# Softmax dealt out in three stages, heads four steps apart, rotary in two steps, retention's first half behind attention

## Chip, cores and metric

One core of a Trainium2 chip runs the whole program. The metric is the device time of one execution in microseconds (us).

## What is computed

One block of a streaming encoder on 256 frames of width 2048: a half-step SwiGLU feed-forward, two token mixers side by side (chunked band attention, retention), gates that merge them, a second feed-forward, a last norm. What the change touches is in the mixers:

```python
h = rmsnorm(x, norm_mix_g)
q_a, k_a, v_a, q_r, k_r, v_r, g_r, gate_a, gate_r = split(h @ w_in)
# attention, 8 heads of 128, per head
p = softmax(where(valid, q_a @ k_a.T * 128**-0.5 + bias[rel_idx], -1e30))
att = p @ v_a
# retention, 8 heads of 128, per head and chunk
q_r, k_r = rotary(q_r), rotary(k_r)
s = (q_r @ k_r.T) * decay
ret = s @ v_r + (state part)          # then divided by its root mean square
ret = silu(g_r) * ret
merged = sigmoid(gate_a) * (att @ w_out_att) + sigmoid(gate_r) * (ret @ w_out_ret)
x = x + merged @ w_out
```

## The kernel before

All large products run in fp32 by three passes: weights and inputs are split into a high and a low half, and TensorE forms hi x hi, hi x lo and lo x hi. The work is a list of **steps**, each a 256-row chunk of a 512-column weight block (two pieces of 128 rows by two tiles of frames by three passes: 12 matmuls). SyncE's queue loads a chunk; `split` (L117 to L124) makes its halves: a cast on ScalarE (L121, `hi`) and a subtraction on VectorE (L122, `lo`). `run` (L220) goes through the steps in order. At step c it first issues the split of step c + 3 (four buffers for each half, `SPLIT_BUFS`), then the side work that is due at c, then the products of c. `later(n, fn)` (L104) puts a piece of side work n steps ahead; `at(step, fn)` puts it at a step. On TensorE a step thus reads [side work][12 products]; on ScalarE and VectorE [split of c + 3][side work]. Nothing reorders this afterwards: what the list says is each engine's order.

PSUM has six banks for the products (tags `acc` and `z`) and a ring of two for side work (`side_tile`, L90), so a third side tile waits until the first has been copied out.

The stretch that the change touches starts with step `mixed` (the second half of retention's value projection), eight steps; then come qr0, kr0, qr1, kr1, eight steps each, then the output projections. Its side work is:

- the relative bias: `set_bias` loads it transposed and, four steps on, turns it with sixteen transposes through four side tiles (`psb`, L325) which ScalarE copies out (L330). It starts at step `mixed`.
- attention, head by head: `scores` (two products `as`, L848, L849; then all of the softmax: scale and bias on VectorE L856, maxima L862, sign L863, the powers on ScalarE L865, reciprocal L868, multiplication L870), two steps later `transposes` (`apt`, L877, with a copy on ScalarE L879), two steps later `values` (`av`, L885, L886, with a split whose low half, `attl`, is on VectorE, L343). Heads are three steps apart; the first has its scores at `mixed` + 10.
- a finished q or k projection of retention: `ret_qk_done` has ScalarE move two tiles out of PSUM (L806), rotates both on VectorE at once (L815 to L818, six operations for each tile), and has them transposed three or four steps later (`qr0p` and the like, L348, copied out by ScalarE L783 and VectorE L785).
- retention, once per half (four heads): `scores` (`rs`, L908, L909; decay on VectorE L911, L912), two steps later `values` (`ro`, L921 to L923), heads two steps apart; one step behind the last `values` stands `finish`, the closing: square on ScalarE (L931), sum on VectorE (L933), reciprocal root with a power on GpSimd (L338, L339), gate on VectorE (L939).
- GpSimd's queue loads the gain of the second norm, gates and decay; the gain is turned by one narrow transpose (L263).

Of the kernel before, what the change touches and what calls it, by code (L numbers as in the profile page):

```python
# [10 lines left out]
AF = mybir.ActivationFunctionType  # L11
# [6 lines left out]
NT = SEQ // P  # L18
# [19 lines left out]
HALF_K = D // P // 2  # L38
LEAD = 12
MIX_LEAD = 8  # L40
HELD = 6

SHARE = (0.85,) * 4 + (1.0,) * 4 + (0.8,) + (0.4,) * 3 + (0.15,) * 4
# [27 lines left out]
def block_kernel(ctx: ExitStack, tc: tile.TileContext, x, g1, w1g, w1u, w1d, gm, w_in, rel, woa, wor, wo,  # L71
                 g2, w2g, w2u, w2d, gf, cos, sin, decay, ident, out):
    nc = tc.nc
# [19 lines left out]
    def tmp_tile(name, tag="t", bufs=None):  # L93
        return tmp.tile([P, NB], F32, tag=tag, name=name, bufs=bufs)
# [9 lines left out]
    def later(n, fn):  # L104
        due.setdefault(state["step"] + n, []).append(fn)
# [649 lines left out]
    nm = Norm("nm", gains[:, 1, :], True)  # L755
# [12 lines left out]
    scale = HD ** -0.5  # L768
# [31 lines left out]
    def ret_qk_done(key, b, after=None):  # L800
        def done(acc):
            srcs = []
            half = HD // 2
            for t in range(NT):
                s = tmp_tile(f"{key}{b}{t}", "gate", 2)
                nc.scalar.activation(s, acc[t], AF.Copy, scale=nm.scale(t))  # L806
                r = tmp_tile(f"{key}{b}{t}r", "qk", 4)
                u = tmp_tile(f"{key}{b}{t}u", "scaled", 1)
                s4 = s.rearrange("p (h j d) -> p h j d", h=4, j=2)
                r4 = r.rearrange("p (h j d) -> p h j d", h=4, j=2)  # L810
                u4 = u.rearrange("p (h j d) -> p h j d", h=4, j=2)
                c = cos_sb[:, t, :].unsqueeze(1).to_broadcast([P, 4, half])
                n = sin_sb[:, t, :].unsqueeze(1).to_broadcast([P, 4, half])
                for j in range(2):
                    nc.vector.tensor_mul(r4[:, :, j, :], s4[:, :, j, :], c)  # L815
                    nc.vector.tensor_mul(u4[:, :, j, :], s4[:, :, 1 - j, :], n)
                nc.vector.tensor_sub(r4[:, :, 0, :], r4[:, :, 0, :], u4[:, :, 0, :])
                nc.vector.tensor_add(r4[:, :, 1, :], r4[:, :, 1, :], u4[:, :, 1, :])  # L818
                srcs.append(r)
            to_transposed(key, b, srcs, 4 if after is None else 3)  # L820
            if after is not None:
                after()

        return done
# [15 lines left out]
    def attention(h):  # L840
        b, i = h // 4, h % 4
        hs = slice(i * HD, (i + 1) * HD)
        sm = {}

        def scores():
            q, k = tposed["qa", b], tposed["ka", b]
            ps = side_tile(f"as{h}")
            nc.tensor.matmul(ps[:, 0:SEQ], q[:, i, P:SEQ], k[:, i, :], start=True, stop=True)  # L848
            nc.tensor.matmul(ps[:, SEQ : SEQ + P], q[:, i, 0:P], k[:, i, 0:P], start=True, stop=True)  # L849
            room = act_tile(F32, f"p{h}").rearrange("p a q -> p (a q)")  # L850
            s = room[:, : 3 * P].rearrange("p (j k) -> p j k", j=3)
            sm["room"] = room
            p3 = ps[:, : 3 * P].rearrange("p (j k) -> p j k", j=3)

            for j, bj in ((0, 1), (1, 0), (2, 0)):
                nc.vector.scalar_tensor_tensor(  # L856
                    s[:, j, :], p3[:, j, :], scale, table["bias", b][:, i, bj * P : (bj + 1) * P], op0=ALU.mult, op1=ALU.add
                )
            m = small.tile([P, NT], F32, tag="m", name="m")
            tot = small.tile([P, NT], F32, tag="l", name="l")  # L860
            for t, js in ((1, slice(0, 2)), (0, slice(2, 3))):
                nc.vector.reduce_max(m[:, t : t + 1], s[:, js, :], axis=AX.XY)  # L862
            nc.vector.tensor_scalar_mul(m, m, -1.0)  # L863
            for t, js in ((1, slice(0, 2)), (0, slice(2, 3))):
                nc.scalar.activation(  # L865
                    s[:, js, :], s[:, js, :], AF.Exp, bias=m[:, t : t + 1], accum_out=tot[:, t : t + 1]
                )
            nc.vector.reciprocal(tot, tot)  # L868
            for t, js in ((1, slice(0, 2)), (0, slice(2, 3))):
                nc.vector.tensor_scalar_mul(s[:, js, :], s[:, js, :], tot[:, t : t + 1])  # L870
            sm["p"] = s

        def transposes():
            ps = side_tile(f"apt{h}")

            for j, c in ((2, 0), (0, 1), (1, 2)):
                nc.tensor.transpose(ps[:, c * P : (c + 1) * P], sm["p"][:, j, :], id_sb)  # L877
            pt = sm.pop("room")[:, 3 * P : 6 * P]
            nc.scalar.copy(pt, ps[:, : 3 * P])  # L879
            sm["pt"] = pt  # L880

        def values():
            v = nat["va", b]
            ps = side_tile(f"av{h}")
            nc.tensor.matmul(ps[:, :SEQ], v[:, 0, hs], sm["pt"][:, :SEQ], start=True, stop=False)  # L885
            nc.tensor.matmul(ps[:, P:SEQ], v[:, 1, hs], sm["pt"][:, SEQ:], start=False, stop=True)  # L886
            hi, lo = att.alloc(b)
            split_out(ps[:, :SEQ], hi[:, i, :], lo[:, i, :])

        return scores, transposes, values  # L890

    def all_attention():
        for h in range(HEADS):
            for s, stage in enumerate(attention(h)):
                later(2 + 3 * h + 2 * s, stage)

    def retention(b):
        outs = {}

        def head(i):  # L900
            h = 4 * b + i
            hs = slice(i * HD, (i + 1) * HD)
            sm = {}

            def scores():
                q, k = tposed["qr", b], tposed["kr", b]
                ps = side_tile(f"rs{h}")
                nc.tensor.matmul(ps[:, 0:SEQ], k[:, i, 0:P], q[:, i, :], start=True, stop=True)  # L908
                nc.tensor.matmul(ps[:, SEQ : SEQ + P], k[:, i, P:SEQ], q[:, i, P:SEQ], start=True, stop=True)  # L909
                s = act_tile(F32, f"rp{h}").rearrange("p a q -> p (a q)")[:, : 3 * P]  # L910
                nc.vector.tensor_mul(s[:, :SEQ], ps[:, :SEQ], table["decay", b][:, i, :])  # L911
                nc.vector.tensor_mul(s[:, SEQ:], ps[:, SEQ : SEQ + P], table["decay", b][:, i, 0:P])  # L912
                sm["s"] = s

            def values():
                if i == 0:
                    for t in range(NT):
                        outs[t] = acc_tile(f"ro{b}{t}", ("acc", "z")[t])
                v = nat["vr", b]
                s = sm["s"]  # L920
                nc.tensor.matmul(outs[0][:, hs], s[:, 0:P], v[:, 0, hs], start=True, stop=True)  # L921
                nc.tensor.matmul(outs[1][:, hs], s[:, P:SEQ], v[:, 0, hs], start=True, stop=False)
                nc.tensor.matmul(outs[1][:, hs], s[:, SEQ:], v[:, 1, hs], start=False, stop=True)  # L923

            return scores, values

        def finish():
            srcs = []
            for t in range(NT):
                sq = tmp_tile(f"rsq{b}{t}", "gate", 2)  # L930
                nc.scalar.activation(sq, outs[t], AF.Square)  # L931
                ms = small.tile([P, 4], F32, tag="ms", name="ms")
                nc.vector.reduce_sum(ms, sq.rearrange("p (h d) -> p h d", h=4), axis=AX.X)  # L933
                rs = small.tile([P, 4], F32, tag="rs", name="rs")
                rsqrt(rs, ms, HD, 4)
                o = tmp_tile(f"rg{b}{t}", "qk", 4)
                for i in range(4):
                    hs = slice(i * HD, (i + 1) * HD)
                    nc.vector.scalar_tensor_tensor(  # L939
                        o[:, hs], outs[t][:, hs], rs[:, i : i + 1], nat["gr", b][:, t, hs], op0=ALU.mult, op1=ALU.mult  # L940
                    )
                srcs.append(o)
            later(3, lambda: [ret.put(b, t, srcs[t]) for t in range(NT)])

        for i in range(4):
            for s, stage in enumerate(head(i)):
                later(5 + 2 * i + 2 * s, stage)
        later(5 + 2 * 4, finish)

    w_in0 = w_in[0]  # L950

# [35 lines left out]
    mixed = len(steps)  # L987
# [14 lines left out]
    merges, of_ret = [], []  # L1002
# [72 lines left out]
    def at(step, fn):  # L1075
        due.setdefault(step, []).append(fn)
# [3 lines left out]
    turn = load_gain(g1, 0, nc.scalar)  # L1080
# [45 lines left out]
    mix = next(c for c, s in enumerate(steps) if s.job.w is w_in0)  # L1126
    at(mix - 18, load_rel)
    at(mix - 14, lambda: later(4, load_gain(gm, 1)))
    at(mixed, set_bias)
    at(mixed + 8, all_attention)  # L1130
    at(mixed + 8, lambda: later(8, load_gain(g2, 2)))
    at(mixed + 16, load_ret_gates)
    at(mixed + 20, set_decay)
    for step, fn in merges:
# [65 lines left out]
```

## Time and profile before

| | |
|---|---|
| median of 3 runs | 2115.38 us (2114.66 to 2119.7) |
| profiled execution | 2116.28 us, span 2114.5 us |
| TensorE busy | 2070.1 us (98% of the span) |
| VectorE busy | 1761.4 us (83%) |
| ScalarE busy | 1407.0 us (67%) |
| GpSimd busy | 273.5 us (13%) |
| mean granted clock of TensorE | 0.996 |

The span runs from the first to the last instruction; the profiled execution's time lies 1.8 us above it. Busy times are over the whole program; the stretch of the change is 1060 to 1280 of the span. In a row of the timeline stand the start, the time of the group, engine, line and operation, output and inputs, their shapes, and in brackets how long the engine had been idle before it and what it waited for. A granted clock of 1.00 is 2.4 GHz, 0.5 is 1.2 GHz.

### The profile page before, as it was taken

Reading aid. Unit: us, or ns where it says so; the run is one execution under the profiler, and the core shown is the slowest. Engines: PE = TensorE matmul, PEld = TensorE weight load, DVE = VectorE, ACT = ScalarE, POOL = GpSimd, SP = SyncE. Lnnn points to the kernel's source line nnn. Section 1 sums busy time; section 2 is a strip of 40 time slices with the busy share of each in tenths; the row PEclk is TensorE's granted clock in tenths of the full one; section 3 lists DMA queues with packets and bytes.
Section 4 is the critical chain, followed back from the end, with each engine's and each line's share of the span. In section 5 each row is a group of like instructions: output and inputs, shape, how many; then the busy total and the mean of one; then the engine's idle time right before and its main releaser. Section 6 shows DMA issues by size and latency. Waiting matters only on the chain. (4 is left out here: it accounts for less than half of the span.)

```text
span 2114.5 us, 25819 instructions
## 1 busy us (share of the span) xinstructions
PE 2070.1 (98%) x9256; PEld 1691.4 (80%) x9256; DVE 1761.4 (83%) x1825; ACT 1407.0 (67%) x1734; POOL 273.5 (13%) x322
## 2 busy tenths in 40 slices
PE   9999999999999999999998999999999999999998
PEld 7788878878888888878787788887888878888886
DVE  6998899889997799888856567568889988898986
ACT  7677667767777766766664334556676677677785
POOL 1111211122111111112100000010121012110200
PEclk9999999999999999999999999999999999999999
DMA  8666876688668677789774455565787668766873
GB/s 299 194 215 231 269 218 203 232 254 252 195 224 264 239 214 228 245 269 291 215 241 142 146 199 189 180 236 173 237 269 226 195 226 269 230 202 225 279 209 130
DMA packets 219314, 473.27 MB, mean 224 GB/s; under 512 B 14817, under 2 KB 15569, under 8 KB 219185
## 3 DMA queue, kind: packets, MB, share of 16 engines
q1 hardware_dynamic: 161376, 310.42, 42.7%
q0 software_dynamic: 54752, 155.88, 27.1%
q10 hardware_dynamic: 3056, 5.32, 0.7%
q8 instruction: 72, 1.18, 0.2%
q14 instruction: 58, 0.47, 0.1%
HBM read 462.65 MB, written 8.91 MB: 223 GB/s over the span
## 5 line engine op out<-in xcount | busy, mean ns | idle before, releaser
L122 DVE TENSOR_TENSOR lo<-raw,hi 128x1024 fp32r<-128x1024 f32 (+1 forms) x401 | 487.2, 1219 | 180.7 <-ACT hi L121 179.1
L121 ACT CAST hi<-raw 128x1024 fp32r<-128x1024 f32 (+1 forms) x401 | 418.7, 1047 | 222.1 <-PE acc L131 135.9
L729 ACT ACTIVATE acc<-xall 128x512 f32<-128x512 f32 x96 | 57.5, 599 | 8.4 <-DVE f2g L696 3.5
L732 ACT ACTIVATE xall<-acc 128x512 f32<-128x512 f32 x96 | 56.4, 588 | 4.5 <-PE acc L131 3.7
L129 PE MATMUL acc<-hi,mgh 128*128 128x512 f32 x128 | 50.2, 392 | 0.0
L131 PE MATMUL acc<-hi,mgl 128*128 128x512 f32 x128 | 49.9, 390 | 0.0
L130 PE MATMUL acc<-lo,mgh 128*128 128x512 f32 x128 | 49.8, 389 | 0.0
L130 PE MATMUL acc<-lo,nma01h 128*128 128x512 f32 x96 | 38.9, 406 | 1.7 <-DVE lo L122 1.7
L129 PE MATMUL acc<-hi,nma01h 128*128 128x512 f32 x96 | 39.4, 411 | 0.0
L129 PE MATMUL acc<-hi,nma00h 128*128 128x512 f32 x96 | 39.3, 409 | 0.0
L130 PE MATMUL acc<-lo,nma00h 128*128 128x512 f32 x96 | 38.4, 401 | 0.3 <-DVE lo L122 0.3
L131 PE MATMUL acc<-hi,nma01l 128*128 128x512 f32 x96 | 38.4, 400 | 0.0
L131 PE MATMUL acc<-hi,nma00l 128*128 128x512 f32 x96 | 38.0, 396 | 0.0
L129 PE MATMUL acc<-hi,nma11h 128*128 128x512 f32 x96 | 37.7, 393 | 0.0
L129 PE MATMUL acc<-hi,nma10h 128*128 128x512 f32 x96 | 37.7, 393 | 0.0
L131 PE MATMUL acc<-hi,nma11l 128*128 128x512 f32 x96 | 37.6, 392 | 0.0
L130 PE MATMUL acc<-lo,nma10h 128*128 128x512 f32 x96 | 37.6, 392 | 0.0
L130 PE MATMUL acc<-lo,nma11h 128*128 128x512 f32 x96 | 37.6, 392 | 0.0
L131 PE MATMUL acc<-hi,nma10l 128*128 128x512 f32 x96 | 37.4, 390 | 0.0
L131 PEld LDWEIGHTS acc<-hi,mgl 128*128 128x128 f32 x128 | 24.0, 188 | 4.9
L130 PEld LDWEIGHTS acc<-lo,mgh 128*128 128x128 f32 x128 | 24.0, 188 | 4.9
L129 PEld LDWEIGHTS acc<-hi,mgh 128*128 128x128 f32 x128 | 24.0, 188 | 4.9
(6130 smaller groups left out, 7149.4 us busy)
## 6 DMA issues: line engine op xcount, KB each, us to landing
raw<-in_ffn_w_down_dram SPq DMA_DIRECT2D x176, 512.0 KB, 6.2
raw<-in_w_in_dram SPq DMA_DIRECT2D x96, 512.0 KB, 4.7
raw<-in_ffn_w_up_dram SPq DMA_DIRECT2D x32, 512.0 KB, 8.5
raw<-in_w_out_dram SPq DMA_DIRECT2D x32, 512.0 KB, 3.5
raw<-in_ffn_w_gate_dram SPq DMA_DIRECT2D x31, 512.0 KB, 4.5
raw<-in_w_out_att_dram SPq DMA_DIRECT2D x16, 512.0 KB, 4.7
raw<-in_w_out_ret_dram SPq DMA_DIRECT2D x16, 512.0 KB, 3.5
z380x<-in_w_in_dram POOLq DMA_DIRECT2D x8, 512.0 KB, 7.8
```

The costliest lines, as they stand in the source:

```text
L121: nc.scalar.copy(hi[:, p, :], raw[:, p, :])
L122: nc.vector.tensor_sub(lo[:, p, :], raw[:, p, :], hi[:, p, :].bitcast(F32))
L129: nc.tensor.matmul(acc, ahi, whi, start=first, stop=False, **more)
L130: nc.tensor.matmul(acc, ahi, wlo, start=False, stop=False, **more)
L131: nc.tensor.matmul(acc, alo, whi, start=False, stop=last, **more)
L729: nc.scalar.activation(acc, xs[t][:, cols], AF.Copy, scale=2.0)
L732: nc.scalar.activation(xs[t][:, cols], acc, AF.Copy, scale=0.5)
```

## The change

Line numbers from L41 on move by one, and behind the rotary by more (L856 becomes L862, L870 becomes L884, L939 becomes L954).

- The softmax is three stages: scores with maxima at 0, powers on ScalarE at 1, shares (reciprocal and multiplication) at 2; transposes at 3, values at 5 (before: 0, 2, 4). Heads are four steps apart in place of three, and the first has its scores at `mixed` + 4 in place of `mixed` + 10.
- The bias is loaded six steps earlier, and so turned at `mixed` - 2 in place of `mixed` + 4.
- Of a rotary projection one tile is rotated in the first step after it, the other in the second; the transposes come four steps after, for all four.
- Retention's first half has its first scores 14 steps after its trigger, its second half 6; both were 5.
- The gain of the second norm is loaded at `mixed` + 44 in place of `mixed` + 8.

```diff
+RET_WAIT = (14, 6)
...
-            for t in range(NT):
-                s = tmp_tile(f"{key}{b}{t}", "gate", 2)
-                nc.scalar.activation(s, acc[t], AF.Copy, scale=nm.scale(t))
+
+            def turn(t, s):
                 r = tmp_tile(f"{key}{b}{t}r", "qk", 4)
...
                 srcs.append(r)
-            to_transposed(key, b, srcs, 4 if after is None else 3)
+
+
+            for t in range(NT):
+                s = tmp_tile(f"{key}{b}{t}", "gate", 2)
+                nc.scalar.activation(s, acc[t], AF.Copy, scale=nm.scale(t))
+                later(1 + t, lambda t=t, s=s: turn(t, s))
+            to_transposed(key, b, srcs, 4)
...
             nc.vector.tensor_scalar_mul(m, m, -1.0)
+            sm["p"], sm["m"], sm["tot"] = s, m, tot
+
+
+        def powers():
+            s, m, tot = sm["p"], sm["m"], sm["tot"]
             for t, js in ((1, slice(0, 2)), (0, slice(2, 3))):
...
+
+        def shares():
+            s, tot = sm["p"], sm["tot"]
             nc.vector.reciprocal(tot, tot)
...
-        return scores, transposes, values
+        return (0, scores), (1, powers), (2, shares), (3, transposes), (5, values)
 
     def all_attention():
         for h in range(HEADS):
-            for s, stage in enumerate(attention(h)):
-                later(2 + 3 * h + 2 * s, stage)
+            for s, stage in attention(h):
+                later(2 + 4 * h + s, stage)
...
-                later(5 + 2 * i + 2 * s, stage)
-        later(5 + 2 * 4, finish)
+                later(wait + 2 * i + 2 * s, stage)
+        later(wait + 2 * 4, finish)
...
-    at(mixed, set_bias)
-    at(mixed + 8, all_attention)
-    at(mixed + 8, lambda: later(8, load_gain(g2, 2)))
+    at(mixed - 6, set_bias)
+    at(mixed + 2, all_attention)
+    at(merges[0][0] + 4, lambda: later(8, load_gain(g2, 2)))
```

The order of VectorE at head 3 and the projection qr0, before. `qr01r` is the second rotated tile, `lo` the low half of a weight chunk, `p` the scores of the head, later its shares.

```order
L817 TENSOR_TENSOR qr01r<-qr01r,qr01u 128x4x64
L818 TENSOR_TENSOR qr01r<-qr01r,qr01u 128x4x64
L122 TENSOR_TENSOR lo_9366<-raw_9224,hi_9365 128x1024
L856 SCALAR_TENSOR_TENSOR p_9378<-as_9375,bias_9048 128x128 x3
L862 TENSOR_REDUCE m<-p_9378 128x1 x2
L863 TENSOR_SCALAR m<-m 128x2
L868 RECIPROCAL l<-l 128x2
L870 TENSOR_SCALAR p_9378<-p_9378,l 128x256
L870 TENSOR_SCALAR p_9378<-p_9378,l 128x128
```

Now, from the weight chunk behind the first rotated tile on:

```order
L123 TENSOR_TENSOR lo_9419<-raw_9274,hi_9418 128x1024
L344 TENSOR_TENSOR attl_9209<-av_9424,atth_9208 128x256
L815 TENSOR_TENSOR qr01r<-qr_9371,cos_sb 128x4x64
L816 TENSOR_TENSOR qr01u<-qr_9371,sin_sb 128x4x64
L815 TENSOR_TENSOR qr01r<-qr_9371,cos_sb 128x4x64
L816 TENSOR_TENSOR qr01u<-qr_9371,sin_sb 128x4x64
L817 TENSOR_TENSOR qr01r<-qr01r,qr01u 128x4x64
L818 TENSOR_TENSOR qr01r<-qr01r,qr01u 128x4x64
L123 TENSOR_TENSOR lo_9452<-raw_9304,hi_9451 128x1024
L882 RECIPROCAL l<-l 128x2
L884 TENSOR_SCALAR p_9387<-p_9387,l 128x256
L884 TENSOR_SCALAR p_9387<-p_9387,l 128x128
```

The head's scores and maxima, which stood behind both rotated tiles, now stand ahead of them, and its shares behind both and two weight chunks.

The order of ScalarE around the copies of the bias, before (`hi` is the high half of a weight chunk, `gr` a gate's transfer to memory):

```order
L121 CAST hi_8961<-raw_8822 128x1024
L970 ACTIVATE sg_8971<-z531a,nmrstd 128x512
L971 DMA gr_104<-sg_8971 128x512
L121 CAST hi_8988<-raw_8860 128x1024
L121 CAST hi_9006<-raw_8927 128x1024
L121 CAST hi_9024<-raw_8941 128x1024
L121 CAST hi_9042<-raw_8953 128x1024
L330 COPY bias_9048<-psb_9050 128x512
L330 COPY bias_9048<-psb_9056 128x512
L330 COPY bias_9049<-psb_9062 128x512
L330 COPY bias_9049<-psb_9068 128x512
```

Now:

```order
L122 CAST hi_8927<-raw_8751 128x1024
L982 ACTIVATE z531c_8895<-z531c_8895 128x512
L986 DMA gr_105<-z531c_8895 128x512
L122 CAST hi_8941<-raw_8780 128x1024
L331 COPY bias_8947<-psb_8949 128x512
L331 COPY bias_8947<-psb_8955 128x512
L331 COPY bias_8948<-psb_8961 128x512
L331 COPY bias_8948<-psb_8967 128x512
```

The copies stood behind three casts in a row of plain steps; now they stand behind one that follows a gate tile (`z531c`) and its transfer.

The order of VectorE at the closing of retention's first half (`ms`, `v`, `rg`), before:

```order
L122 TENSOR_TENSOR lo_10029<-raw_9853,hi_10028 128x1024
L933 TENSOR_REDUCE ms<-rsq_10041 128x4
L338 TENSOR_SCALAR v<-ms 128x4
L939 SCALAR_TENSOR_TENSOR rg_10049<-ro_9826,rs,gr_9371 128x128 x4
L933 TENSOR_REDUCE ms<-rsq_10054 128x4
L338 TENSOR_SCALAR v<-ms 128x4
L939 SCALAR_TENSOR_TENSOR rg_10062<-ro_9827,rs,gr_9371 128x128 x4
L122 TENSOR_TENSOR lo_10080<-raw_9909,hi_10079 128x1024
```

Now, with `rp` the decayed scores of the second half's first head:

```order
L123 TENSOR_TENSOR lo_10239<-raw_10090,hi_10238 128x1024
L948 TENSOR_REDUCE ms<-rsq_10247 128x4
L339 TENSOR_SCALAR v<-ms 128x4
L954 SCALAR_TENSOR_TENSOR rg_10255<-ro_10058,rs,gr_9380 128x128 x4
L948 TENSOR_REDUCE ms<-rsq_10260 128x4
L339 TENSOR_SCALAR v<-ms 128x4
L954 SCALAR_TENSOR_TENSOR rg_10268<-ro_10059,rs,gr_9380 128x128 x4
L926 TENSOR_TENSOR rp_10276<-rs_10273,decay_9515 128x256
L927 TENSOR_TENSOR rp_10276<-rs_10273,decay_9515 128x128
```

A weight chunk followed the closing; now the decay product of the second half does.

## Rows read from the trace of the kernel before

**Rows 1.** TensorE's waits by line, 1060 to 1420: line, releaser, total, count, longest

```profile
PE kr0p L348 <- DVE attl L343: 3.6, 1, 3.6
PE apt L877 <- DVE attl L343: 3.0, 1, 3.0
PE qr0p L348 <- DVE p L856: 2.0, 1, 2.0
PE av L885 <- DVE p L856: 1.6, 1, 1.6
PE qr1p L348 <- ACT qr1T L783: 0.8, 1, 0.8
PE psb L325 <- ACT bias L330: 0.7, 1, 0.7
```

**Rows 2.** table of stretches: length, busy (count) by engine, clock, DMA share, GB/s

```profile
1120.00:1130.00 10.00, 8.41 (x40) 6.66 (x39) 8.07 (x21) 3.87 (x9) 0.00 (x0) 1.00 0.35 110
1130.00:1140.00 10.00, 7.96 (x36) 6.61 (x35) 3.89 (x13) 3.61 (x8) 0.00 (x0) 0.83 0.40 131
```

**Rows 3.** timeline of TensorE at qr0p (start, length, line, operation, idle before)

```profile
1133.85 1.09 PE L348 MATMUL qr0p<-id_sb,qr01r 128*128 128x128 f32 x4 [2.04 <-DVE p L856]
...
1138.65 0.59 PE L885 MATMUL av<-p,va 128*128 128x256 f32 x2
```

**Rows 4.** timeline, a plain step on TensorE, ScalarE and VectorE

```profile
1072.03 0.39 PE L129 MATMUL acc<-hi,nma00h 128*128 128x512 f32 x1
...
1074.75 0.39 PE L129 MATMUL acc<-hi,nma01h 128*128 128x512 f32 x1
...
1074.95 1.05 ACT L121 CAST hi<-raw 128x1024 fp32r<-128x1024 f32 x1 [1.13 <-PE acc L131]
...
1076.04 1.23 DVE L122 TENSOR_TENSOR lo<-raw,hi 128x1024 fp32r<-128x1024 f32 x1 [0.96 <-ACT hi L121]
```

**Rows 5.** timeline of TensorE, a step with av (head 1 to 2)

```profile
1111.94 0.59 PE L885 MATMUL av<-p,va 128*128 128x256 f32 x2
...
1115.34 0.49 PE L877 MATMUL apt<-id_sb,p 128*128 128x128 f32 x3
```

**Rows 6.** timeline at head 3 and qr0: TensorE, ScalarE, VectorE

```profile
1118.43 0.59 PE L848 MATMUL as<-ka0T,qa0T 128*128 128x256 f32 x2
...
1119.21 1.04 ACT L121 CAST hi<-raw 128x1024 fp32r<-128x1024 f32 x1
...
1117.99 0.42 DVE L815 TENSOR_TENSOR qr00r<-qr,cos_sb 128x256 f32<-128x256 f32 x1
...
1122.02 1.22 DVE L122 TENSOR_TENSOR lo<-raw,hi 128x1024 fp32r<-128x1024 f32 x1
1123.16 0.68 DVE L856 SCALAR_TENSOR_TENSOR p<-as,bias 128x128 f32<-128x128 f32 x3
...
1124.39 0.17 DVE L863 TENSOR_SCALAR m<-m 128x2 f32<-128x2 f32 x1
```

**Rows 7.** timeline of VectorE, shares of an ordinary head

```profile
1113.46 0.17 DVE L868 RECIPROCAL l<-l 128x2 f32<-128x2 f32 x1 [1.05 <-ACT p L865]
...
1114.40 1.23 DVE L122 TENSOR_TENSOR lo<-raw,hi 128x1024 fp32r<-128x1024 f32 x1 [0.19 <-ACT hi L121]
```

**Rows 8.** timeline of ScalarE, casts after the gate tile, and bias copies

```profile
1068.74 2.95 ACT L121 CAST hi<-raw 128x1024 fp32r<-128x1024 f32 x3 [0.45 <-ACT z531c L967]
...
1082.68 1.07 ACT L330 COPY bias<-psb 128x512 f32<-128x512 f32 x2 [0.26 <-PE psb L325]
```

**Rows 9.** timeline of VectorE at retention's closing, of TensorE at ro with rs

```profile
1210.31 1.23 DVE L122 TENSOR_TENSOR lo<-raw,hi 128x1024 fp32r<-128x1024 f32 x1 [3.15 <-ACT hi L121]
...
1217.58 3.48 DVE L122 TENSOR_TENSOR lo<-raw,hi 128x1024 fp32r<-128x1024 f32 x3
...
1179.51 0.39 PE L921 MATMUL ro<-vr,rp 128*128 128x128 f32 x2
...
1183.60 0.59 PE L848 MATMUL as<-ka1T,qa1T 128*128 128x256 f32 x2
```

More of the change, by code (lines that the diff above doesn't have):

```diff
@@ L870, in scores @@
                 nc.vector.tensor_scalar_mul(s[:, js, :], s[:, js, :], tot[:, t : t + 1])
-            sm["p"] = s
         def transposes():
@@ L888, in values @@
             split_out(ps[:, :SEQ], hi[:, i, :], lo[:, i, :])
-        return scores, transposes, values
+        return (0, scores), (1, powers), (2, shares), (3, transposes), (5, values)
     def all_attention():
         for h in range(HEADS):
-            for s, stage in enumerate(attention(h)):
-                later(2 + 3 * h + 2 * s, stage)
+            for s, stage in attention(h):
+                later(2 + 4 * h + s, stage)
     def retention(b):
+        wait = RET_WAIT[b]
         outs = {}
```

## Prediction

> **What bounds the kernel now.** I read the page's busy times first: TensorE 98% of the span, VectorE 83%, ScalarE 67%. A change in the order of side work can only win what TensorE loses, so the next view was TensorE's waits in the stretch that the change touches: six waits of 11.7 us in all [rows 1] and a seventh of 0.3, every one at side work of the mixers and none at a weight. The larger ones end on VectorE: transposes of rotated heads (kr0p, qr0p), a transpose or a product of the softmax (apt, av). The third view is the table of stretches: the granted clock is 1.00 in 1120 to 1130, which holds the stall of 1.6 (av), and 0.83 in 1130 to 1140, which holds that of 2.0 (qr0p) [rows 2]. So more is lost than the idle time: after the 2.04 TensorE ran at half clock (1.2 in place of 2.4 GHz), and the step took from 1133.85 to 1138.65, 4.80 us [rows 3]. The 12 products of a plain step take 2.72 [rows 4]; av with its products takes 3.40, so that av and the change of operands cost 0.68 [rows 5], and four transposes a little less: this step would have lasted about 3.2, and 1.6 are lost. The stalls of 3.6 and 3.0 are followed by the same clock and the same loss. Within a run of products one starts 0.23 after the other, while a record lasts 0.39, so each stall delays by 0.16 more than its idle time. **Lost in the mixers now:** 12.0 + 7 x 0.16 + 3 x 1.6 = 17.9. That is the most that the change can win, 0.85% of the time.
>
> **The clockwork of a step.** TensorE begins a plain step at 1074.75. ScalarE's cast of the weights that are due three steps on starts 0.20 later, released by TensorE's last product of the step before (a buffer comes free); VectorE's subtraction for them starts at 1076.04, 1.29 after the step's start [rows 4]. Both stand ahead of the step's side work on their engines. What VectorE does for a step thus ends no earlier than 1.29 + 1.14 (a subtraction, 1122.02 to 1123.16 [rows 6]) + its own time after TensorE began that step. The change deals work out by whole steps, so whether a stage is ready one step on is this sum against 2.72.
>
> **The change, part by part.** The instructions and their sizes stay on every engine; only places move.
>
> *Softmax, ordinary heads (five: 0, 1, 2, 4, 6).* The powers go to ScalarE a step after the scores. VectorE no longer waits for them (1.05 idle per head now [rows 7]); that is worth nothing by itself, since VectorE then waits for the next cast instead. The shares stand in the step before the transposes, behind that step's subtraction. Reciprocal and two multiplications take 0.75 (1113.46 to 1114.40, less 0.19 idle [rows 7]). They end 1.29 + 1.14 + 0.75 = 3.18 after the step's start, and TensorE is at the transposes after 2.72. With 0.06 to wake it, **0.52 is lost per head, 2.6 in all**, where these heads lose nothing now.
>
> *Rotary heads (three: head 3 with qr0, 5 with kr0, 7 with qr1).* The projection ends where the head's scores are due. ScalarE moves its two tiles out of PSUM first, so the cast starts 0.78 after the step (1118.43 to 1119.21 [rows 6]) and the subtraction 1.09 behind it, as in [rows 4] (1074.95 to 1076.04): 1.87. From there VectorE runs without a gap up to the shares: subtraction 1.14; scores, maxima and sign 1.23 + 0.20 (1123.16 to 1124.39, and that row); first rotary half 2.02 (half of 1117.99 to 1122.02 [rows 6]); subtraction 1.14; the low half of the head before 0.34 (as long as a sixth of 2.02); second rotary half 2.02; subtraction 1.14; shares 0.75. The sum is 9.98, the end 11.85 after the scores' step began. TensorE's three steps before the transposes take 3.40 (scores, of the shapes of av), 3.40 (av) [rows 5] and 2.72: 9.52. With the same 0.06 it waits 2.39, some 2.2 of it as idle time. The second tile's transposes share a PSUM bank with apt and wait for ScalarE's copy of that, at most 0.54 (half of 1.07, a wider copy [rows 8]), less what the first tile's transposes cover: about 0.37. **2.76 per head, 8.3 in all**; these three places lose 2.0, 3.6 and 3.0 now, before the clock. The rotary in two steps serves a low half between them, but leaves the shares last.
>
> *Bias transposes, six steps earlier.* They land in the step that begins at 1074.75 - 3 x 2.72 = 1066.59. Eight of the sixteen transposes fill the two PSUM banks; the others wait for ScalarE's copies, which here stand behind a cast that starts only at 1068.74 (the row's three casts are 0.95 apart; ahead of them a gate tile waits for VectorE [rows 8]). The first copy ends at 1068.74 + 0.95 + 0.55 = 1070.24, the products begin at about 1071.23, 4.64 after the step's start; without the wait it would be 1.72 for sixteen transposes at 0.43 per four. **2.9 lost, 2.7 as idle time**; now it is 0.7 + 0.16 [rows 1].
>
> *kr1's two tiles* are transposed alone in a step, both through one bank, as qr1's now: the second waits for the copy of the first, **0.8** like qr1p [rows 1].
>
> *Retention's first half* starts 14 steps after its trigger, behind attention. Its closing work holds VectorE from one subtraction at 1210.31 to the next at 1217.58 [rows 9], so to 1.29 + 7.27 = 8.56 after its step's start. That work now stands ahead of the decay product of the second half's first head, which comes in the same step and needs 0.4 more: 8.96. TensorE wants it two steps on, after one step with retention's products and scores of 4.09 (1179.51 to 1183.60 [rows 9]) and one of 2.72: 6.81. **2.2 lost, 2.0 as idle time.** The subtractions queued behind are needed three steps on; that cover hides them, and if it is gone TensorE waits at a weight, by up to 1 us.
>
> *Gain and gate loads:* a transfer and one narrow transpose move, and POOL's queue takes these loads ahead of the reciprocal roots, for which only the closing work waits. Between 0 and 0.3; I take 0, their buffers being long free.
>
> **The sum.** 2.6 + 8.3 + 2.9 + 0.8 + 2.2 = 16.8 of stalls, against 12.0 + 1.1 = 13.1 now: 3.7 more. Half clock costs 4.8 now, later 1.6 for each of n falls, so the difference is 3.7 - 4.8 + 1.6 n = -1.1 + 1.6 n. Five of the new stalls can lower the clock: idle 2.7, three times 2.2, 2.0. The nearest rows say that 1.6 did not and 2.0 did [rows 1, 2]; close above such a point I take four of five: **+5.3**. The profiled execution took 2116.28; the median of the runs shown is 2115.38, 0.9 below. On the median this is **2120.7**. Bounds of the terms: 0.2 for an ordinary head (the wake-up), 1 for a rotary head, 0.5 for the bias, 1 for retention, each way.
>
> The Trainium skill, TensorE: Matmul & The Clock Gate, section "HAM oscillation — how this bites in real kernels", has an abstract rule by which the clock falls only for idle gaps longer than any of mine. By that rule n is 0 and the time 2114.3. The trace does not agree: the gaps of 3.0 and of 2.0 were both followed by half clock.
>
> **Rivals.**
> 1. *Faster: the shares come in time.* If the casts are released earlier than I assume, so that VectorE's subtractions run ahead, the five waits of 0.5 and the three of 2.4 vanish. It decides from half a microsecond per ordinary head. Left are 2.9 + 0.8 + 2.2 + 3 x 0.37 = 7.0 of stalls and about 1.5 falls of the clock, 2.4: 9.4 in place of 17.9, which gives 2106.9. For it: VectorE is given back 1.05 of idle time per head. Against it: the cast's release by the product of the step before, which the waiting of [rows 4] shows. 0.12.
> 2. *Slower: half clock after all five.* One mechanism: at each stall of 2.0 or more TensorE resumes at 1.2 GHz, as it did behind the 2.0 of qr0p. n = 5 gives -1.1 + 8.0 = +6.9, 2122.3; with one term at its upper bound, 2123.5. It decides from whether retention's 2.0, the shortest, still lowers the clock. 0.25.
> 3. *The clock hardly falls* (n from 0 to 2, the 2.2 and 2.0 lying close above a 1.6 that did nothing): 2114.3 to 2117.5. The kernel has traded waits for waits and the change does nothing that shows. 0.18.
> 4. *My forecast*, three or four falls: 2119.1 to 2120.7. 0.45.
>
> **How the numbers follow.** A measurement of this kernel can tell 0.3%, 6.3 us, from no change: below 2109.0 is faster, above 2121.7 slower. Faster: rival 1, and 0.01 of tails, 0.13. Slower: rival 2, 0.25. Same: the rest, 0.62. The range leaves out the better half of rival 1 and what lies above rival 2 with one term at its bound: 2107 to 2124.
>
> **What would show it.** Right: TensorE's waits list apt five times at about 0.4 and three times at about 2.2 behind VectorE's shares, psb at about 2.7 behind ScalarE's bias copy, ro at about 2.0 behind the decay product; the clock is 0.83 in four stretches of ten microseconds; the waits of qr0p, kr0p and av are gone but for the copies' 0.4. Wrong: apt without waits (rival 1), those stalls with the clock at 1.00 (rival 3), in five of them below it (rival 2), or a wait at a weight's subtraction, the cover I counted on.

## The result and the profile after

The changed kernel takes 2120.96 us (median of 14 runs, 2116.86 to 2124.53), the kernel before, timed beside it, 2116.77 (14 runs, 2113.39 to 2119.7): a ratio of 1.0021, 95% interval [1.0013, 1.003]. The interval lies above 1, so this is a small loss; by the bound of the prediction (0.3%) it counts as no change. The difference is 4.2, where 5.3 was forecast. The profiled execution took 2121.39, its span is 2119.6.

The page of the changed kernel, busy times (compare the table ahead of the prediction): the same work.

```profile
PE 2070.2 (98%) x9256; PEld 1692.1 (80%) x9256; DVE 1760.7 (83%) x1825; ACT 1407.4 (66%) x1734; POOL 273.3 (13%) x322
```

TensorE's waits by line, 1060 to 1420, which answer to [rows 1]:

```profile
PE apt L890 <- DVE p L884: 9.3, 8, 2.2
PE psb L326 <- ACT bias L331: 2.7, 1, 2.7
PE ro L936 <- DVE rp L926: 2.1, 1, 2.1
PE kr1p L349 <- ACT kr1T L784: 0.7, 1, 0.7
```

None of the old waits at qr0p, kr0p and av is left. There are eight at apt in their place, and the three at psb, ro and kr1p that the sum had. The total is 14.8 now, 12.0 before.

The table of stretches for TensorE (length, busy and count by engine, clock, DMA share, GB/s), which answers to [rows 2]; a fall that lies across two stretches shows in both:

```profile
1070.00:1080.00 10.00, 10.00 (x42) 8.52 (x43) 4.55 (x6) 5.27 (x7) 0.00 (x0) 0.85 0.58 169
1130.00:1140.00 10.00, 7.85 (x37) 6.29 (x36) 8.71 (x20) 4.54 (x10) 0.53 (x1) 0.90 0.66 209
...
1170.00:1180.00 10.00, 10.00 (x44) 8.28 (x44) 4.67 (x10) 3.42 (x8) 0.53 (x1) 0.90 0.44 129
...
1200.00:1210.00 10.00, 10.00 (x45) 8.40 (x44) 3.35 (x4) 2.95 (x4) 1.03 (x2) 0.86 0.46 142
...
1240.00:1250.00 10.00, 7.95 (x43) 6.46 (x42) 7.41 (x18) 2.47 (x3) 1.65 (x2) 1.00 0.35 114
```

Four falls: behind psb (1070), and behind apt of heads 3, 5 and 7 (from 1137, 1168 and 1199 on). The stretch with the wait at ro, 1240 to 1250, is at 1.00.

An ordinary head (the second), timeline of VectorE and TensorE (start, length, engine, line, operation, idle before and its releaser), against [rows 4, 7]:

```profile
1107.17 1.23 DVE L123 TENSOR_TENSOR lo<-raw,hi 128x1024 fp32r<-128x1024 f32 x1 [1.88 <-ACT hi L122]
...
1108.50 0.55 DVE L884 TENSOR_SCALAR p<-p,l 128x256 f32<-128x256 f32 x2
```

```profile
1109.20 0.52 PE L890 MATMUL apt<-id_sb,p 128*128 128x128 f32 x3 [0.48 <-DVE p L884]
```

The step of the shares begins on TensorE at 1105.84. The subtraction starts 1.33 later, the shares end at 1108.50 + 0.55 = 1109.05, 3.21 after the step's start, and TensorE goes on 0.15 after that. The first head waits longer, 0.96; there ScalarE loads a table ahead of the powers:

```profile
1090.64 1.28 ACT L876 ACT_TABLE_LOAD   x1
```

The first rotary head (head 3, qr0), against [rows 6]:

```profile
1127.43 1.23 DVE L123 TENSOR_TENSOR lo<-raw,hi 128x1024 fp32r<-128x1024 f32 x1 [3.05 <-ACT hi L122]
...
1133.37 0.42 DVE L815 TENSOR_TENSOR qr01r<-qr,cos_sb 128x256 f32<-128x256 f32 x1
...
1136.71 0.55 DVE L884 TENSOR_SCALAR p<-p,l 128x256 f32<-128x256 f32 x2
```

```profile
1125.57 0.59 PE L854 MATMUL as<-ka0T,qa0T 128*128 128x256 f32 x2
...
1137.40 0.52 PE L890 MATMUL apt<-id_sb,p 128*128 128x128 f32 x3 [2.15 <-DVE p L884]
...
1143.08 0.60 PE L854 MATMUL as<-ka1T,qa1T 128*128 128x256 f32 x2
```

VectorE has no gap from 1127.43, 1.86 after TensorE began the scores' step, to the end of the shares at 1137.26, 11.7 after it. TensorE waits 2.15 for them. Its step then lasts from 1137.40 to 1143.08.

The bias, timeline of ScalarE and TensorE, against [rows 8]:

```profile
1068.34 1.04 ACT L122 CAST hi<-raw 128x1024 fp32r<-128x1024 f32 x1 [0.45 <-ACT z531c L982]
1069.29 1.07 ACT L331 COPY bias<-psb 128x512 f32<-128x512 f32 x2
```

```profile
1069.92 1.97 PE L326 MATMUL psb<-id_sb,biasT 128*128 128x128 f32 x8 [2.69 <-ACT bias L331]
```

Gate tile, transfer, cast, and only then the copies for which half of the transposes wait: 2.69.

The closing of retention's first half, VectorE and TensorE, against [rows 9]:

```profile
1243.73 1.13 DVE L954 SCALAR_TENSOR_TENSOR rg<-ro,rs,gr 128x128 f32<-128x128 f32 x4 [1.12 <-POOL rs L340]
1244.77 0.42 DVE L926 TENSOR_TENSOR rp<-rs,decay 128x256 f32<-128x256 f32 x1
```

```profile
1236.23 0.38 PE L936 MATMUL ro<-vr,rp 128*128 128x128 f32 x2
...
1245.24 0.49 PE L936 MATMUL ro<-vr,rp 128*128 128x128 f32 x2 [2.06 <-DVE rp L926]
```

The decay product starts at 1244.77, 8.54 after the step began at 1236.23 and right behind the closing's last gate; TensorE waits 2.06 for it.

### The profile page after: what moved, and what is told of

Same layout as the page of the kernel before. It is cut to its first block, busy times and chain, and to the rows that moved or that the text cites. A ratio compares the mean times of both kernels' runs of the same rounds, so it can differ in the third digit from the quotient of the medians.

```text
span 2119.6 us, 25816 instructions
## 1 busy us (share of the span) xinstructions
PE 2070.2 (98%) x9256; PEld 1692.1 (80%) x9256; DVE 1760.7 (83%) x1825; ACT 1407.4 (66%) x1734; POOL 273.3 (13%) x322
## 4 chain that ended last, share of the span: by engine, by line
PE 75%; DVE 11%; issue 4%; ACT 4%; DMA 3%; ACTq 0%; POOL 0%; POOLq 0%; DVEq 0%
PE acc L131 14%; PE acc L132 14%; PE acc L130 14%; DVE lo L123 3%; DMA raw<-in_ffn_w_down_dram 2%; ACT hi L122 1%; DMA z992x<-in_ffn_w_gate_dram 1%; DMA raw<-in_w_in_dram 1%; PE z380a L130 0%; PE z128a L131 0%; PE z128a L130 0%; PE z380a L132 0%; PE z380a L131 0%; PE z684a L130 0%; PE z89a L131 0%
```

## The experiments

Every edit is against the changed kernel (2120.96) unless it says otherwise; ratios are against the kernel before, timed on the same chip. The experiments ran on three chips, and the changed kernel was not timed again beside them. A figure "below the changed kernel" is therefore a difference of medians from different sets of runs; the kernel before had medians from 2115.3 to 2116.8 in them, so such a figure is good to some 2.

**1. Transposes and values one step later.**

```diff
-        return (0, scores), (1, powers), (2, shares), (3, transposes), (5, values)
+        return (0, scores), (1, powers), (2, shares), (4, transposes), (6, values)
```

> Transposes of the shares and the values each one step later (stages 0, 1, 2, 4, 6), nothing else. My theory (the shares are a step too near to the transposes: shares end 3.2 after a step's start of 2.72, and 11.9 after the scores' step against 9.5): all eight waits at apt go (0.96, four of 0.48, three of 2.15, each with 0.16 of delay: 10.6), and the three falls of the clock behind them (1.6 each, 4.8): some 15.4 below the changed kernel's 2121, so 2105.6; left are psb 2.7, ro 2.1, kr1p 0.7. Rival (VectorE as a whole is short of time in this stretch, so that a wait taken away comes back at the next place): the waits move to qr0p, kr0p or to a weight's low half, and the time stays above 2114.

Measured: 2106.7 (2104.01 to 2106.98), ratio 0.9951 [0.9938, 0.9965], 14.3 below the changed kernel. TensorE's waits of this run, 1060 to 1420:

```profile
PE psb L326 <- ACT bias L331: 2.7, 1, 2.7
PE ro L936 <- DVE rp L926: 2.1, 1, 2.1
PE kr1p L349 <- ACT kr1T L784: 0.7, 1, 0.7
...
PE qr0p L349 <- DVE attl L344: 0.6, 1, 0.6
```

(kr0p and qr1p stand there with the same 0.6.) All eight waits at apt are gone. Of the rival a little is true: 0.6 at each of the second rotated tiles, behind attl. VectorE and TensorE at the first of them:

```profile
1130.88 0.42 DVE L818 TENSOR_TENSOR qr01r<-qr01r,qr01u 128x256 f32<-128x256 f32 x1
...
1132.35 0.42 DVE L344 TENSOR_TENSOR attl<-av,atth 128x256 fp32r<-128x256 f32 x1
```

```profile
1132.83 0.66 PE L349 MATMUL qr0p<-id_sb,qr01r 128*128 128x128 f32 x4 [0.60 <-DVE attl L344]
```

That is not VectorE's time for the rotary: the second tile is ready at 1131.30, 0.93 before TensorE begins to wait. By the order of the side tiles its transposes need the one that the values took a step earlier, whose low half (attl) stands behind the rotary and ends at 1132.77, 0.06 before TensorE goes on; experiment 9 tests it. Three times 0.6 and 0.16 are 2.3; 15.4 less 2.3 would be 13.1, and 14.3 were measured.

**2. Bias three steps later.**

```diff
-    at(mixed - 6, set_bias)
+    at(mixed - 3, set_bias)
```

> The bias is loaded three steps later than in the change (turned in the first plain step behind the gate tile, still ahead of the first head), nothing else. My theory (the first bias copy stands behind a cast that waits behind a gate tile): the wait at psb falls from 2.7 to about 0.8 and the half clock behind it is gone: 1.9 + 1.6, so 2117.5. Rival (the transposes come before the loaded bias has landed, or the copies wait for ScalarE anyway): psb stays above 2 and the time at 2121.

Measured: 2117.25 (2113.71 to 2120.8, 11 runs), ratio 1.0002 [0.9994, 1.0011], 3.7 below the changed kernel, 3.5 expected. The wait at psb is 1.3, not 0.8, and no half clock follows it:

```profile
PE psb L326 <- ACT bias L331: 1.3, 1, 1.3
```

This run shows something else too. The three waits at apt of the rotary heads have the same length, yet here the clock fell behind two of them only (stretches 1130 to 1140, 1160 to 1170, 1190 to 1200):

```profile
1130.00:1140.00 10.00, 7.72 (x41) 6.16 (x39) 6.67 (x14) 3.53 (x5) 0.00 (x0) 1.00 0.63 197
1160.00:1170.00 10.00, 7.86 (x34) 6.42 (x33) 6.10 (x14) 2.84 (x4) 0.00 (x0) 0.83 0.54 159
1190.00:1200.00 10.00, 7.85 (x34) 6.41 (x33) 6.80 (x14) 3.17 (x4) 0.00 (x0) 0.83 0.64 210
```

```profile
1135.03 0.52 PE L890 MATMUL apt<-id_sb,p 128*128 128x128 f32 x3 [2.14 <-DVE p L884]
1135.38 0.60 PE L349 MATMUL qr0p<-id_sb,qr00r 128*128 128x128 f32 x4
1136.11 0.66 PE L349 MATMUL qr0p<-id_sb,qr01r 128*128 128x128 f32 x4
```

**3. Retention's first half one step earlier.**

```diff
-RET_WAIT = (14, 6)
+RET_WAIT = (13, 6)
```

> Retention's first half one step earlier (13 in place of 14), nothing else. My theory (its closing stands ahead of the second half's first decay product in VectorE's queue and ends 2.2 too late): with one step more the decay product ends 9.0 after that step where TensorE needs it after about 9.3; the wait at ro of 2.1 goes, 2.2 less, 2118.8. Rival (the closing holds VectorE wherever it stands): ro or kr1's transposes wait as long, 2121.

Measured: 2118.57 (2116.65 to 2120.79, 11 runs), ratio 1.0011 [1.0002, 1.0019], 2.4 below the changed kernel. The waits of this place:

```profile
PE retp L349 <- DVE rp L927: 1.0, 1, 1.0
PE ro L936 <- DVE rp L926: 0.4, 1, 0.4
```

The median is as expected (2.2 less), the waits are not: ro still waits 0.4, since one subtraction now stands between closing and decay product; kr1p's 0.7 is gone (a head's scores, a third side tile for two banks, no longer share its step); and a wait of 1.0 at retp is new, where the transposes of the gated first half now share a step with scores of the second. From 2.1 + 0.7 to 0.4 + 1.0 is 1.4 less, not 2.2, so that the median agrees in part by luck; the intervals of this run and of the changed kernel overlap.

**4. The three edits together.**

> All three of the edits: transposes and values a step later, bias three steps later, retention's first half a step earlier. My theory: the gains add, 10.6 + 1.9 + 2.2 of waits and 6.4 of half clock, 21.1 below 2121: about 2100, with kr1p 0.7 and psb 0.8 left and the clock at 1.00 throughout. That is 0.8% below the kernel before. Rival (VectorE is short): 2110 or more, with new waits at weights or transposes.

Measured: 2102.87 (2100.65 to 2103.07), ratio 0.9934 [0.9921, 0.9946], 18.1 below the changed kernel. The three single gains are 14.3 + 3.7 + 2.4 = 20.4. What is missing to the 21.1 expected stands in its waits:

```profile
PE psb L326 <- ACT bias L331: 1.3, 1, 1.3
PE retp L349 <- DVE rp L927: 1.0, 1, 1.0
PE qr0p L349 <- DVE attl L344: 0.6, 1, 0.6
...
PE ro L936 <- DVE rp L926: 0.4, 1, 0.4
```

With kr0p and qr1p, which wait 0.6 each too, 4.5 in all where 1.5 was expected, and no half clock in this stretch. There is no new wait at a weight, and the time is far below the rival's 2110: VectorE as a whole is not short of time here.

**5. The rotary in one piece.**

```diff
-                later(1 + t, lambda t=t, s=s: turn(t, s))
+                later(1, lambda t=t, s=s: turn(t, s))
```

> The changed kernel with both rotated tiles worked out in the first step after their projection, as one piece; all else as in the change. My theory (the wait at apt of a rotary head is set by the sum of VectorE's work between two fixed steps, 9.98, and not by its order): the three waits stay at 2.15, the clock falls as often, 2121. Rival (it is the split of the rotary, which puts its second half between the scores and the shares of a head, that makes the shares late): the waits at apt shrink by up to 2.0 and the time falls to 2111 to 2115.

Measured: 2120.54 (2117.0 to 2123.97), ratio 1.0023 [1.0014, 1.0033]. Eight waits at apt as before, three of 2.15:

```profile
PE apt L890 <- DVE p L884: 9.3, 8, 2.2
```

The split of the rotary is worth nothing here, for good or ill. What counts is the sum of VectorE's work between the projection's end and the transposes.

**6. The softmax in one piece, at the new places.**

```diff
             sm["p"], sm["m"], sm["tot"] = s, m, tot
+            powers()
+            shares()
...
-        return (0, scores), (1, powers), (2, shares), (3, transposes), (5, values)
+        return (0, scores), (3, transposes), (5, values)
```

> The changed kernel with the softmax in one piece again, in the step of the scores, as in the kernel before; heads four steps apart, transposes three and values five steps behind the scores, as in the change. My theory: an ordinary head's shares end 1.3 + 1.1 + 1.4 + 1.05 + 0.75 = 5.6 after its scores' step, where TensorE needs them after 9.5, so the five small waits at apt go (3.7 with their delay); at the rotary heads the shares now stand ahead of the rotary, and the second rotated tile is late in their place: 1.87 + 9.98 - 1.14 (the subtraction that stood ahead of the shares) + 1.05 = 11.8 against 10.3, a wait of about 1.5 at qr0p, kr0p and qr1p. 5.6 less waiting, and the clock falls less often behind 1.5 than behind 2.15: 2110 to 2115. Rival (the eight waits come from the heads' new places and not from the three stages): apt waits as now, 2121 or more, since VectorE also waits 1.05 for the powers again.

Measured: 2110.43 (2107.74 to 2114.75, 10 runs), ratio 0.9977 [0.9967, 0.9987], 10.5 below the changed kernel.

```profile
PE qr0p L349 <- DVE qr01r L818: 1.4, 1, 1.4
```

No wait at apt; the rotated tiles wait 1.4 each (kr0p and qr1p as this row), 1.5 expected, and the clock fell behind none of the three (the only half clock of this stretch follows psb). So the rest of the change, the heads' new places with it, is a gain of 0.23% by itself, and the three stages of the softmax, with the transposes one step behind the shares, turn it into a loss. It is not the three stages as such: with the transposes two steps behind the shares (experiment 1) they are faster than the softmax in one piece.

**7. TensorE kept at work in the wait.**

```diff
             ps = side_tile(f"apt{h}")
+            if h in (3, 5, 7):
+                for _ in range(16):
+                    nc.tensor.transpose(ps[:, 0:P], id_sb, id_sb)
```

> The changed kernel with 16 more transposes of the unit matrix on TensorE, ahead of the transposes of the shares of heads 3, 5 and 7, into the same PSUM tile, which is overwritten. They take about 0.11 each, 1.7 of the 2.15 that TensorE waits there. The shares come no earlier, so the wait's end stays where it was. My theory (the half clock behind the wait comes from TensorE having nothing to do, and costs 1.6 each time): idle 0.4 ahead of apt, granted clock 1.00 behind it at all three, 4.8 less, 2116. Rival (the half clock costs nothing, since the step behind it is waited for anyway, or it does not come from the idle time): 2121 and the clock falls as before.

Measured: 2115.86 (2114.02 to 2118.87, 11 runs), ratio 1.0005 [0.9996, 1.0014], 5.1 below the changed kernel, 4.8 expected. Stretches and the first place:

```profile
1130.00:1140.00 10.00, 9.57 (x57) 8.01 (x56) 9.20 (x24) 5.33 (x10) 0.53 (x1) 1.00 0.65 192
...
1160.00:1170.00 10.00, 9.57 (x56) 7.95 (x55) 9.20 (x22) 4.74 (x10) 0.00 (x0) 1.00 0.54 156
1190.00:1200.00 10.00, 9.57 (x56) 7.95 (x55) 8.66 (x19) 4.12 (x9) 0.46 (x1) 1.00 0.67 216
```

```profile
1135.97 1.91 PE L890 MATMUL apt<-id_sb 128*128 128x128 f32 x16
1138.18 0.55 PE L893 MATMUL apt<-id_sb,p 128*128 128x128 f32 x3 [0.30 <-DVE p L884]
...
1142.53 0.59 PE L854 MATMUL as<-ka1T,qa1T 128*128 128x256 f32 x2
```

The shares come as late as before, the transposes wait until the same time, and the clock is 1.00 at all three places. From the end of the wait to the next head's scores it is 4.35 here, 5.68 in the changed kernel, 1.33 less; at heads 5 and 7 it is 1.25 less each, 3.8 in all. By the ratios to the kernel before (1.0021 and 1.0005) the gain is 3.4; the 5.1 compares two sets of runs, in which the kernel before itself differs by 1.4 (2116.77 and 2115.35). So some 4 of the 18 that separate the changed kernel from experiment 4 are half clock behind these three waits, and not the idle time itself.

**8. Experiment 4 with the heads two steps later.**

```diff
-RET_WAIT = (14, 6)
+RET_WAIT = (13, 6)
...
-        return (0, scores), (1, powers), (2, shares), (3, transposes), (5, values)
+        return (0, scores), (1, powers), (2, shares), (4, transposes), (6, values)
...
-    at(mixed - 6, set_bias)
-    at(mixed + 2, all_attention)
+    at(mixed, set_bias)
+    at(mixed + 4, all_attention)
```

> The three edits of the last run (transposes and values a step later, first half of retention a step earlier, bias later), and the heads all two steps later, so that a head's scores no longer fall into the step behind a projection; the bias is loaded at the step where the kernel before loads it. My theory: VectorE's work from the projection's end to the second rotated tile is 1.87 + 1.14 + 0.75 + 2.02 + 1.14 + 2.02 = 8.9 where TensorE needs it after 9.5, so the three waits of 0.6 at qr0p, kr0p and qr1p go (0.76 each), psb falls from 1.3 to 0.8: 2.8 below the last run's 2102.9, 2100. Rival (with two side tiles in PSUM the transposes and retention's first products now meet in the same steps, and wait for each other): 2103 or more.

Measured: 2103.87 (2101.62 to 2104.75), ratio 0.9945 [0.9932, 0.9958]: nothing won over experiment 4, 2.8 less was expected. psb falls to 0.8 as expected. But the second rotated tile still waits 0.6, now for `p` of the scores' step:

```profile
PE qr0p L349 <- DVE p L862: 0.6, 1, 0.6
```

My account of VectorE's time was right (the rotated tile is ready in time), and the cause is of the rival's kind, a PSUM side tile, though not retention's: the one that the transposes take was the scores' a step earlier. VectorE reads the scores (L862) from 1130.98 to 1131.66, behind both rotated tiles and a weight chunk, and the transposes start at 1131.81.

**9. Experiment 4 with the values five steps behind the scores, and the bias two steps later still.**

```diff
-        return (0, scores), (1, powers), (2, shares), (3, transposes), (5, values)
+        return (0, scores), (1, powers), (2, shares), (4, transposes), (5, values)
...
-RET_WAIT = (14, 6)
+RET_WAIT = (13, 6)
...
-    at(mixed - 6, set_bias)
+    at(mixed - 1, set_bias)
```

> As the run with all three edits, but the values again five steps behind the scores (one behind the transposes), and the bias turned two steps later still, at the step ahead of the first head. My theory (the waits of 0.6 at qr0p, kr0p and qr1p are for a PSUM side tile that a head's values took one step earlier, and whose low half stands on VectorE behind the second rotated tile and a weight chunk): with the values a step earlier that low half stands ahead of the second rotated tile, the tile is free in time and the tile itself ready 0.4 before TensorE needs it; three times 0.76 go, and psb falls from 1.3 to 0.8: 2.8 below the 2102.9 of that run, about 2100. Rival (VectorE is now the bound of this stretch): the waits move to the values, which have one step less for the copy of the transposed shares, or to qr0p behind the rotary: 2103 or more.

Measured: 2099.72 (2098.86 to 2102.95), ratio 0.9929 [0.9915, 0.9943] against 2115.3 of the kernel before. All of TensorE's waits from 1060 to 1420:

```profile
PE retp L349 <- DVE rp L927: 1.0, 1, 1.0
PE psb L326 <- ACT bias L331: 0.7, 1, 0.7
PE ro L936 <- DVE rp L926: 0.4, 1, 0.4
```

The three waits at the rotated tiles are gone: attl now ends before the second tile is turned, and that tile is ready at 1129.00, 0.43 before TensorE takes it up. So it was the side tile. In time the lead over experiment 4 is not clear of noise (0.9929 and 0.9934); it is the waits that show it, 2.1 in place of 4.5. This version beats both kernels: 0.71% below the one before, 21.2 us below the changed one by the medians (19.5 by the ratios), by other numbers in the table of steps, with the same products and operations.

## Why the prediction was right

The time was forecast as 2120.7 and is 2120.96; the sum of stalls as 16.8, of which the changed kernel's trace has 14.8 as idle time and 11 x 0.16 = 1.8 as the matmuls' overlap, 16.6. The mechanism is the one forecast, wait by wait, but that both totals agree so closely is luck in part. In the sum the ordinary heads were put 1.1 too low and the rotary heads 1.4 too high. The time was reached from a kernel before at 2115.38, which beside the changed one measured 2116.77: as a difference 5.3 was forecast and 4.2 measured (5.1 between the two profiled executions). Step by step:

- **What can be lost and won.** The loss in the mixers was put at 17.9 and called the most that can be won. Experiment 9 won 15.6 (2115.3 to 2099.72), and 2.1 of waits are left in the stretch.
- **Ordinary heads, 0.52 each.** Idle 0.48 and 0.16 of delay, 0.64: the shares end where the sum had them (3.18 forecast, 3.21), but TensorE starts 0.15 after them, not 0.06. The first head waits 0.96, which no term had. Behind the table load ahead of its powers the next cast starts 0.75 after its step began, not 0.24, and the subtraction ahead of the shares is late by about as much. With this head the five cost 3.7, where 2.6 was forecast. Experiment 1, which gives the stage a step more, takes all of it away.
- **Rotary heads.** 2.2 of idle time forecast, 2.15 measured at all three. The wait of 0.37 for the PSUM bank behind apt was put too high and its place in the sum overlaps: where the clock does not fall it is 0.30 (experiment 2, 1135.38 to 1136.11, less the 0.43 of four transposes); where it falls, the first tile's transposes are so slow that it is hidden. With 2.15 and 0.16 the three cost 6.9, where 8.3 was forecast. Experiments 5 and 6 show that the cause is the sum of VectorE's work between two fixed steps: one order or the other makes the shares or the second tile late.
- **Bias: 2.7 forecast, 2.69. Retention: 2.0 against 2.06.** Experiments 2 and 3 take them away or down; what came in their place (1.3; 0.4 and 1.0) was sized too low in what was expected of these runs. One thing was not looked at: while the closing holds VectorE (1238.65 to 1244.77), VectorE stands idle 1.15 and 1.12 for GpSimd's two reciprocal roots, together more than TensorE's 2.06. No run fills these gaps.
- **kr1's two tiles: 0.8 forecast, 0.68 and 0.16.** The size is right, one word of the reason is not: they are not alone in their step. The scores of a head of retention (`rs`) are the step's first side tile, so that the second of the transposed tiles is the third for two banks. Experiment 3, in which the scores fall into the step before, has no wait there.
- **The cover counted on.** No wait at a weight's low half is new in this stretch; three steps of preparation were enough. The moved loads, taken at 0, cause no wait there either.
- **Half clock.** Four falls of five forecast, four in the profiled execution; the one that did not come is ro, the shortest. Experiment 7 shows that idle time is the cause at apt. Against it the three falls cost 1.33, 1.25 and 1.25; since the wait of 0.30 for the bank is back at full clock, a fall by itself costs some 1.6, as forecast, and the forecast counted both at each rotary head. The count of four was a choice and came true in this execution. A wait of 2.14 lowers the clock in one place and not in another (experiment 2), and the 14 runs of the changed kernel have mean clocks from 0.994 (2124.53) to 0.997 (2116.86). So the number of falls seems to change from one execution to the next; only one execution of each kernel has a trace that would show it.

Of the rivals, the first (the shares come in time) is excluded by the eight waits at apt, the second (five falls) by ro in the execution that was traced. The third, that the clock hardly falls, may be what the fastest single run did: 2116.86, with a mean clock of 0.997. The rule of the Trainium skill that was weighed (TensorE: Matmul & The Clock Gate, "HAM oscillation — how this bites in real kernels") does not hold in this kernel: gaps of 2.15 and 2.69 were followed by half clock, and filling the gaps of 2.15 took it away.

Left open: with which idle time the clock falls. The traces show 2.06 (changed kernel) without, 2.04 (kernel before) with, 2.14 (experiment 2) with and without, and none of 1.6 or less that did.

## What to carry to other kernels

Where work is dealt out in whole steps to engines that each run in order, work out for every stage when its engine can begin it in its step and when it is done, and compare that with the step's length: half a microsecond too much is lost at each of its repetitions, and one step more costs nothing as long as buffers last. Splitting a long stage helps only if the pieces that others wait for do not end up behind the rest; the sum of work on the busy engine between two fixed points stays. And a wait that is gone shows the next one: here a side tile in PSUM, held by a stage that stood behind in another engine's queue.

## What was not expected of the hardware

The same wait of 2.14 to 2.15, at the same three places of the program, is followed by half clock at eleven of twelve places in four traces (changed kernel, experiments 2, 3 and 5) and by full clock at one. The runs of the changed kernel spread over 7.7 us, and the slowest has the lowest mean clock; that such falls make the spread is not shown, since experiment 6, whose waits at these places are 1.4 and lower no clock, spreads over 7.0. Filling idle time with work whose result is thrown away won some 4 us at three places, though no share came sooner.
